# A two-layer decoder trunk on one core: a mask and its row count, PSUM pools and buffers of the two token mixers changed

## The chip, the cores and the metric

The kernel runs on one core of one Trainium2 chip. The metric is the device time of one execution in microseconds. Three executions of the kernel before took 2031.06, 2037.0 and 2038.48 us; their median is 2037.0.

## What is computed

x is 512 tokens by 1024, in float32. The reference runs two layers; each is half a feed-forward block, a token mixer, half a feed-forward block, and a layer norm after each of the three. The even layer's mixer is RG-LRU beside mLSTM, the odd layer's is RWKV-7 beside GLA.

```python
for l in range(DEPTH):
    x = layer_norm(alpha * x + 0.5 * swiglu_ffn(x, ffn1_wi[l], ffn1_wo[l]), ...)
    if l % 2 == 0:
        mix = even_mixer(x, ...)   # RG-LRU and mLSTM, one input and one output projection
    else:
        mix = odd_mixer(x, ...)    # RWKV-7 and GLA, likewise
    x = layer_norm(alpha * x + mix, ...)
    x = layer_norm(alpha * x + 0.5 * swiglu_ffn(x, ffn2_wi[l], ffn2_wo[l]), ...)
```

In the mLSTM part, a score between tokens i and j is weighted by exp of a gate difference, and j > i is masked out. RWKV-7 is a recurrence over tokens with a 64 x 64 state for each of 8 heads; GLA is a linear attention with 4 heads and a gate of its own.

## The kernel before

**Precision and weights.** Every large product is made of three: each float32 operand is split into a rounded part (hi) and the rest (lo), both of type float32r, and hi by hi, lo by hi and hi by lo are added in PSUM. `load` (L87) fetches 512 KB of weights into one of two `raw` buffers; `split` (L95) makes `whi` on ScalarE (L103) and `wlo` on VectorE (L107), or, in most of the odd mixer, on ScalarE (L105) and by an adding DMA (L110). There are five slots of each. `project_T` (L127) makes a projection of 128 outputs by 512 tokens with 16 products by whi (L132, L133) and 8 by wlo (L136); `project_N` (L148) does the same for four token tiles (L156 to L158).

**PSUM.** `psum` (L83) hands out banks of 128 x 512 from three pools: A has four buffers, B two, C two. An allocation takes a pool's buffers in turn, so it waits until the reader of the buffer's last use is done.

**Order.** A scheduler places the instructions of each engine. In the odd mixer `fill` (L658) also puts a number of steps of waiting projections (`filler`) in at marked places; the numbers are the table `FILL` (L25), one for each call of `fill` in the program's order. An engine works through its instructions in the order set.

**First mixer** (`even`, L318). The order is: `if` projection and four of the eight query and key projections (`pqk`) in two halves of 256 tokens, the other four in full (L433), each followed by a convolution of one step on ScalarE (L313) and three on VectorE (L316) that read the PSUM buffer; then the scores, the value projection (`pv`, L441), RG-LRU and the output. For one head and one block of 128 keys, `scores` (L414) makes a gate matrix `pr` of up to 512 columns in pool B. A product with 36 rows does it (L420): `sel` picks the head's row out of `Rs`, which holds 32 rows of hi parts and 4 of lo parts. A second product adds the mask (L421): the identity by a triangle of -1e30, both in bf16. ScalarE takes exp (L423), TensorE makes `pS` from keys and queries (L425), VectorE multiplies the two (L427). There are 16 such groups, mixed by the scheduler with the projections that follow.

**Second mixer** (`odd`, L567). RWKV-7 is handled in four blocks of 128 channels, two to a group. For each block, `keys` (L687) makes the decay product `pw` (L693) and the key gate product `pa` (L697), each with 32 rows, the norm `pn` (L706), which GpSimd raises to a power (L709), and a broadcast of it, `pi` (L732), after which VectorE builds `KRV` and `bk`. `bonus` (L740) makes `pb` with one more product. All of them use pool B, as `pl` does, the gate product of GLA (L933). Six buffers named `wk` hold what lies between. Then, for each group, `scores` (L746, `psc` L755), `inverse` (L786, 31 steps on VectorE between L792 and L801), `natural` (L762, transposes `ptk` and `ptb`, and `pz`), `merge` (L805, `pq`, `px`, `pwt`, `pu`) and `chain` (L850): eight chunks, one after another, in each of which `psa` (L864) reads the state that VectorE made from `pst` (L872) of the chunk before. GLA's projections (`pj`, `pv`, `po`, all in pool A) fill in.

**Second mixer, buffers of GLA's gates.** `gla_gates` (L928) takes four `wk` buffers for two channel blocks (`zb`, `za`), and the results go into the two buffers `ga`. `gwt` (L593), a 256-column weight, has a buffer of its own beside the `wk` pool.

Of the kernel before, what the change touches and what calls it, by code (L numbers as in the profile page):

```python
# [7 lines left out]
F32 = mybir.dt.float32  # L8
# [3 lines left out]
ALU = mybir.AluOpType  # L12
# [23 lines left out]
class Net:  # L36
# [281 lines left out]
    def even(self, l):  # L318
        nc, a, tc = self.nc, self.a, self.tc
        V, A, T, G = nc.vector, nc.scalar, nc.tensor, nc.gpsimd  # L320
        with tc.tile_pool(name="ev", bufs=1) as ep:
            bufs = dict(qk=8, row=4, wt=3, v=4, u=4, rg=6, o=6)

            def slot(tag, n=S):
                return ep.tile([P, 516 if tag == "v" else S], F32, name=tag, tag=tag, bufs=bufs[tag])[:, :n]
# [8 lines left out]
            msk = ep.tile([P, 2, P], BF, name="msk")  # L334
            mtmp = slot("wt", 256)
            nc.sync.dma_start(mtmp.rearrange("p (a b) -> p a b", a=2), a["c_mask_neg"])
            V.tensor_copy(out=msk, in_=mtmp.rearrange("p (a b) -> p a b", a=2))
# [52 lines left out]
            Rs = ep.tile([36, 1280], F32R, name="Rs")  # L390
            sel = ep.tile([36, 4], F32R, name="sel")
# [22 lines left out]
            def scores(h):  # L414
                pT = ep.tile([P, 1280], F32, name=f"pT{h}", tag="pT", bufs=4)
                out, off = [], 0
                for bj in range(4):
                    n = S - bj * P
                    pr = self.psum("pr")
                    T.matmul(pr[:, :n], sel[:, h:h + 1].broadcast_to([36, P]), R[bj], start=True, stop=False)  # L420
                    T.matmul(pr[:, :P], msk[:, 0, :], msk[:, 1, :], start=False, stop=True)  # L421
                    wt = slot("wt")
                    A.activation(wt[:, :n], pr[:, :n], AF.Exp, bias=cT[:, bj, h:h + 1])  # L423
                    pS = self.psum("pS")
                    T.matmul(pS[:, :n], qk[4 + h][:, bj * P:(bj + 1) * P], qk[h][:, bj * P:], start=True, stop=True)  # L425
                    o = pT[:, off:off + n]
                    V.scalar_tensor_tensor(out=o, in0=pS[:, :n], scalar=128 ** -0.5, in1=wt[:, :n], op0=ALU.mult, op1=ALU.mult)  # L427
                    out.append(o)
                    off += n
                return out  # L430


            for i in order[4:]:  # L433
                p_qk[i] = self.psum("pqk", "A")
                self.project_T(p_qk[i], self.weights())
                qk_tile(i)
# [130 lines left out]
    def odd(self, l):  # L567
# [6 lines left out]
        wk = tc.alloc_tile_pool(name="wk", bufs=6, side="right", reuse_waits="tile")  # L574
        with tc.tile_pool(name="od", bufs=1) as ep:
# [17 lines left out]
            gwt = wk.tile([80, 256], F32, name="gwt", bufs=1)  # L593
# [93 lines left out]
            def keys(ft, Dm, k, r, v):  # L687
# [4 lines left out]
                pw = self.psum("pw")  # L692
# [3 lines left out]
                pa = self.psum("pa")  # L696
# [43 lines left out]
            def bonus(ft, r, v):  # L740
                pb = self.psum("pb")
                T.matmul(pb, bones, r, start=True, stop=True)
                yT[ft] = slot("y")
                V.tensor_tensor(out=yT[ft], in0=v, in1=pb, op=ALU.mult)
# [183 lines left out]
            def gla_gates():  # L928

                zz = []  # L930
                for f in range(2):
                    pl = self.psum("pl")
                    T.matmul(pl, gw[:, f * P:(f + 1) * P], gd[0:80], start=True, stop=True)  # L933
                    zb, za = slot("wk"), slot("wk")
# [7 lines left out]
                for zb, za in zz:  # L942
                    V.scalar_tensor_tensor(out=zb, in0=zb, scalar=0.0, in1=za, op0=ALU.min, op1=ALU.add)
                    gbs.append(slot("ga"))
                    V.tensor_tensor_scan(out=gbs[-1], data0=reset, data1=zb, initial=0.0, op0=ALU.mult, op1=ALU.add)
# [230 lines left out]
def layouts(inp):  # L1176
# [45 lines left out]
    mk = np.zeros((P, 2, P), f)  # L1222
    mk[:, 0] = np.eye(P)
    mk[:, 1] = np.where(np.arange(P)[None, :] < np.arange(P)[:, None], -1e30, 0.0)
# [65 lines left out]
```

## Time and profile before

| | |
|---|---|
| median of three runs | 2037.0 us |
| profiled execution | 2036.15 us |
| its span in the trace | 2034.4 us |
| granted TensorE clock, mean | 0.993 |
| feed-forward block before the first mixer, from 0 to 375 us | TensorE busy 371.89 us |
| from 577 to 1342 us (two feed-forward blocks) | TensorE busy 764.42 us |
| from 1640 to the end | TensorE busy 385.59 us |

The profile is of one execution. Engines are PE (TensorE's products), PEld (its weight loads), DVE (VectorE), ACT (ScalarE), POOL (GpSimd) and SP (SyncE, which issues most DMAs). A row of the view in order of time gives the start, the duration, the engine, the line, the operation with out<-in and its shape, and in square brackets the idle time of the engine before it with what ended it. Products overlap, so TensorE's speed is read from the distance of starts, not from durations. A float32 product (not float32r) shows as two records, so its counts are twice those of the order of instructions. Page part 2 shows how the busy share and the clock run over the span, in 40 slices:

```profile
PE   9999999999999999999999999998999999999998
...
DVE  4332333776784333335533333466747683323335
ACT  4332332466424322332432233157635333322330
...
PEclk9999999999999999999999999998999999999999
```

The two stretches in which VectorE and ScalarE have high digits are the two mixers. TensorE is high throughout.

### The profile page before, as it was taken

To read this page: it belongs to the slowest core of one execution; us is meant where nothing else is said; L and a number is where in the kernel's file an instruction comes from. 1 tells how busy PE (TensorE), PEld (TensorE's weight loads), DVE (VectorE), ACT (ScalarE), POOL (GpSimd) and SP (SyncE) were. 2 spreads that over 40 slices of the span, in tenths; PEclk is the share of its full clock that TensorE was granted. 3 is DMA by queue.
4 is the path that set the end of the run, shared out by engine and by line. 5 is a ranking of instruction groups with operands and counts; after the bars stand their busy time and mean duration, and the time that the engine had idled before them with its cause. 6 is when DMAs were issued, how large, how long until landed. Compare 5 with 4: busy or idle time off the path is not lost. (4 is left out here: it accounts for less than half of the span.)

```text
span 2034.4 us, 26090 instructions
## 1 busy us (share of the span) xinstructions
PE 2008.5 (99%) x10499; PEld 1666.0 (82%) x10499; DVE 964.2 (47%) x1800; ACT 719.6 (35%) x1266; POOL 98.4 (5%) x159
## 2 busy tenths in 40 slices
PE   9999999999999999999999999998999999999998
PEld 8888888977889888888988888896778788888886
DVE  4332333776784333335533333466747683323335
ACT  4332332466424322332432233157635333322330
POOL 0000000100010000000000000012211200000001
PEclk9999999999999999999999999998999999999999
DMA  5333333332223323331433333254636023333331
GB/s 168 103 93 116 102 93 93 94 97 63 73 80 118 103 94 114 104 94 53 130 99 93 114 104 95 84 163 104 144 69 157 1 85 113 98 99 115 99 97 63
DMA packets 59482, 202.45 MB, mean 100 GB/s; under 512 B 7824, under 2 KB 8288, under 8 KB 59360
## 3 DMA queue, kind: packets, MB, share of 16 engines
q1 hardware_dynamic: 56336, 189.77, 30.2%
q0 software_dynamic: 3024, 11.01, 2.9%
q8 instruction: 82, 1.34, 0.3%
q14 instruction: 40, 0.33, 0.1%
HBM read 196.56 MB, written 4.19 MB: 99 GB/s over the span
## 5 line engine op out<-in xcount | busy, mean ns | idle before, releaser
L103 ACT ACTIVATE whi<-raw 128x512 fp32r<-128x512 f32 x661 | 379.6, 623 | 821.0 <-PE pgu L133 401.9
L107 DVE TENSOR_TENSOR wlo<-raw,whi 128x512 fp32r<-128x512 f32 x616 | 398.9, 687 | 541.4 <-ACT whi L103 515.5
L132 PE MATMUL pgu<-xh,whi 128*128 128x512 f32 (+1 forms) x1568 | 564.8, 369 | 1.5 <-ACT whi L103 1.2
L133 PE MATMUL pgu<-xl,whi 128*128 128x512 f32 (+1 forms) x1568 | 565.7, 368 | 0.0
L136 PE MATMUL pgu<-xh,wlo 128*128 128x512 f32 (+1 forms) x1568 | 353.7, 368 | 0.0
L132 PEld LDWEIGHTS pgu<-xh,whi 128*128 128x128 f32 x1568 | 295.3, 189 | 50.7 <-ACT whi L103 1.6
L133 PEld LDWEIGHTS pgu<-xl,whi 128*128 128x128 f32 x1568 | 296.4, 189 | 48.4
L136 PEld LDWEIGHTS pgu<-xh,wlo 128*128 128x128 f32 x1568 | 275.8, 189 | 48.6
L165 PE MATMUL acc<-whi,hh 128*128 128x512 f32 x704 | 274.6, 390 | 0.0
L166 PE MATMUL acc<-whi,hl 128*128 128x512 f32 x704 | 274.4, 390 | 0.0
L167 PE MATMUL acc<-wlo,hh 128*128 128x512 f32 x704 | 272.4, 390 | 0.0
L243 DVE TENSOR_TENSOR sg<-sg,pgu 128x512 f32<-128x512 f32 (+1 forms) x96 | 61.7, 643 | 336.5 <-PE pgu L136 332.8
L167 PEld LDWEIGHTS acc<-wlo,hh 128*128 128x128 f32 x704 | 132.2, 188 | 27.2
L165 PEld LDWEIGHTS acc<-whi,hh 128*128 128x128 f32 x704 | 132.2, 188 | 27.2
L166 PEld LDWEIGHTS acc<-whi,hl 128*128 128x128 f32 x704 | 132.2, 188 | 27.1
L170 ACT ACTIVATE hh<-sg 128x512 fp32r<-128x512 f32 (+1 forms) x96 | 57.2, 596 | 120.7 <-DVE sg L243 120.7
L200 POOL TENSOR_SCALAR rs<-mv 128x1 f32<-128x1 f32 x24 | 13.2, 548 | 1510.7 <-DVE mv L198 1510.7
L242 ACT ACTIVATE sg<-pgu 128x512 f32<-128x512 f32 (+1 forms) x96 | 53.7, 560 | 57.0 <-PE pgu L136 56.3
L170 ACT ACTIVATE xh<-pst 128x512 fp32r<-128x512 f32 x48 | 27.8, 597 | 108.3 <-PE pst L178 108.0
L132 PE MATMUL pj<-xh,whi 128*128 128x512 f32 (+2 forms) x184 | 63.2, 363 | 0.0
L171 DVE TENSOR_TENSOR hl<-sg,hh 128x512 fp32r<-128x512 f32 (+1 forms) x96 | 61.6, 642 | 0.6 <-ACT hh L170 0.5
L133 PE MATMUL pj<-xl,whi 128*128 128x512 f32 (+2 forms) x184 | 61.4, 351 | 0.0
(350 smaller groups left out, 2009.5 us busy)
## 6 DMA issues: line engine op xcount, KB each, us to landing
raw<-ffn_wi SPq DMA_DIRECT2D x176, 512.0 KB, 3.5
raw<-ffn_wo SPq DMA_DIRECT2D x88, 512.0 KB, 3.5
raw<-od_krv SPq DMA_DIRECT2D x12, 512.0 KB, 3.8
raw<-ev_qk SPq DMA_DIRECT2D x8, 512.0 KB, 3.6
raw<-ev_rg SPq DMA_DIRECT2D x8, 512.0 KB, 3.5
raw<-ev_w_out SPq DMA_DIRECT2D x8, 512.0 KB, 3.5
raw<-od_w_out SPq DMA_DIRECT2D x8, 512.0 KB, 4.2
wlo<-od_krv POOLq DMA_DIRECT2D x6, 512.0 KB, 7.1
```

Of the source, the lines that this page charges most:

```text
L103: self.nc.scalar.activation(hi[:, sl], t[:, sl], AF.Copy)
L107: self.nc.vector.tensor_tensor(out=lo[:, sl], in0=t[:, sl], in1=hi[:, sl].bitcast(F32), op=ALU.subtract)
L132: mm(o, hi[:, kt, :n], self.xh[:, kt, t0:t1], start=kt == 0, stop=False)
L133: mm(o, hi[:, kt, :n], self.xl[:, kt, t0:t1], start=False, stop=lo is None and kt == 7)
L136: mm(o, lo[:, kt, :n], self.xh[:, kt, t0:t1], start=False, stop=kt == 7)
L165: mm(o, ah, hi[:, cs], start=first and i == 0, stop=False)
L166: mm(o, al, hi[:, cs], start=False, stop=False)
L167: mm(o, ah, lo[:, cs], start=False, stop=last and i == len(lhs) - 1)
L170: self.nc.scalar.activation(hi, src, AF.Copy)
L171: self.nc.vector.tensor_tensor(out=lo, in0=src, in1=hi.bitcast(F32), op=ALU.subtract)
L242: nc.scalar.activation(sg, pp[f, 0][:, t0:t1], AF.Silu)
L243: nc.vector.tensor_tensor(out=sg, in0=sg, in1=pp[u][:, t0:t1], op=ALU.mult)
```

## The change

The first mixer: the mask becomes one 128 x 128 triangle of type float32r, and the identity by which it is multiplied is a float32r copy of the identity that is there already. `Rs` and `sel` grow from 36 to 128 rows; ScalarE fills rows 32 to 127 with zeros first (a constant scaled by 0), and rows 32 to 35 get their values afterwards, as before. So the product for `pr` has 128 rows, of which 92 are zero. The fifth and sixth projection for `pqk` take their PSUM buffers from pool C, and the last two take the next two of pool A.

The second mixer: `pw`, `pa`, `pb` and `pl` take PSUM buffers from pool A (four) and leave pool B (two) to `pn`, `pi` and what follows. There are seven `wk` buffers for six; `gwt` is one of them, no longer a buffer of its own; `zb` lies in a `ga` buffer and is worked on in place, so `gla_gates` needs two `wk` buffers for four. In `FILL` the number ahead of the last chunk's `psa` in the first group's chain goes from 0 to 2, and one in the second group's `natural` from 9 to 7.

```diff
-    3, 1, 2, 2, 3, 2, 1, 3, 2, 1, 0, 1, 1, 3, 0, 0, 6, 3, 3, 5, 6, 4, 2, 9, 0, 1, 17, 7, 5, 1, 2, 2,
+    3, 1, 2, 2, 3, 2, 1, 3, 2, 1, 2, 1, 1, 3, 0, 0, 6, 3, 3, 5, 6, 4, 2, 7, 0, 1, 17, 7, 5, 1, 2, 2,
...
-            msk = ep.tile([P, 2, P], BF, name="msk")
-            mtmp = slot("wt", 256)
-            nc.sync.dma_start(mtmp.rearrange("p (a b) -> p a b", a=2), a["c_mask_neg"])
-            V.tensor_copy(out=msk, in_=mtmp.rearrange("p (a b) -> p a b", a=2))
+            msk = ep.tile([P, P], F32R, name="msk")
+            mtmp = slot("wt", P)
+            nc.sync.dma_start(mtmp, a["c_mask_neg"])
+            V.tensor_copy(out=msk, in_=mtmp)
+            idr = ep.tile([P, P], F32R, name="idr")
+            V.tensor_copy(out=idr, in_=self.ident)
...
-            Rs = ep.tile([36, 1280], F32R, name="Rs")
-            sel = ep.tile([36, 4], F32R, name="sel")
+            Rs = ep.tile([P, 1280], F32R, name="Rs")
+            sel = ep.tile([P, 4], F32R, name="sel")
+
+            A.activation(Rs[32:64].rearrange("p (a b) -> p a b", a=10), self.expo[32:64].unsqueeze(2).broadcast_to([32, 10, P]), AF.Copy, scale=0.0)
+            A.activation(Rs[64:128].rearrange("p (a b) -> p a b", a=10), self.expo[64:128].unsqueeze(2).broadcast_to([64, 10, P]), AF.Copy, scale=0.0)
+            A.activation(sel[32:64], self.expo[32:64].broadcast_to([32, 4]), AF.Copy, scale=0.0)
+            A.activation(sel[64:128], self.expo[64:128].broadcast_to([64, 4]), AF.Copy, scale=0.0)
...
-                    T.matmul(pr[:, :n], sel[:, h:h + 1].broadcast_to([36, P]), R[bj], start=True, stop=False)
-                    T.matmul(pr[:, :P], msk[:, 0, :], msk[:, 1, :], start=False, stop=True)
+                    T.matmul(pr[:, :n], sel[:, h:h + 1].broadcast_to([P, P]), R[bj], start=True, stop=False)
+                    T.matmul(pr[:, :P], idr, msk, start=False, stop=True)
...
-                p_qk[i] = self.psum("pqk", "A")
+                p_qk[i] = self.psum("pqk", "C" if i in order[4:6] else "A")
...
-        wk = tc.alloc_tile_pool(name="wk", bufs=6, side="right", reuse_waits="tile")
+        wk = tc.alloc_tile_pool(name="wk", bufs=7, side="right", reuse_waits="tile")
...
-            gwt = wk.tile([80, 256], F32, name="gwt", bufs=1)
+            gwt = slot("wk")[:80, :256]
...
-                pw = self.psum("pw")
+                pw = self.psum("pw", "A")
...
-                pa = self.psum("pa")
+                pa = self.psum("pa", "A")
...
-                pb = self.psum("pb")
+                pb = self.psum("pb", "A")
...
-                    pl = self.psum("pl")
+                    pl = self.psum("pl", "A")
...
-                    zb, za = slot("wk"), slot("wk")
+                    zb, za = slot("ga"), slot("wk")
...
-                    gbs.append(slot("ga"))
-                    V.tensor_tensor_scan(out=gbs[-1], data0=reset, data1=zb, initial=0.0, op0=ALU.mult, op1=ALU.add)
+                    gbs.append(zb)
+                    V.tensor_tensor_scan(out=zb, data0=reset, data1=zb, initial=0.0, op0=ALU.mult, op1=ALU.add)
```

How the scheduler then sets TensorE's instructions, at three places. The first is in the first mixer, behind the last projection for `pqk`; - is before, + is the change, and L427, L428 and L432 are the former L420, L421 and L425:

```order
 L136 MATMUL pqk<-xh,wlo 128x512 x8
-L420 MATMUL pr<-Rs,sel 128x512
-L421 LDWEIGHTS msk
-L421 MATMUL pr<-msk 128x128
-L425 MATMUL pS<-qk 128x512
+L156 MATMUL pv<-whi,xh 128x512
+L157 MATMUL pv<-whi,xl 128x512
+L158 MATMUL pv<-wlo,xh 128x512
+L156 MATMUL pv<-whi,xh 128x512
+L427 MATMUL pr<-Rs,sel 128x512
+L428 MATMUL pr<-msk,idr 128x128
+L432 MATMUL pS<-qk 128x512
```

Four products of the value projection move ahead of the first `pr` group.

The second is in the second mixer, from the last products of the first group's scores to the first transposes, before:

```order
L693 MATMUL pw<-lt,lw 128x512
L755 MATMUL psc<-KRV,bk 128x128 x8
L136 MATMUL pj<-xh,wlo 128x512 x8
L697 MATMUL pa<-lt,lw 128x512
L755 MATMUL psc<-KRV,bk 128x128 x8
L706 MATMUL pn<-cst,wk 128x2 x4
L768 MATMUL ptk<-ident,KRV 128x128 x4
```

And in the change, where `psc` is L762 and `ptk` L775:

```order
L133 MATMUL pj<-xl,whi 128x512
L762 MATMUL psc<-KRV,bk 128x128 x8
L136 MATMUL pj<-xh,wlo 128x512 x8
L762 MATMUL psc<-KRV,bk 128x128 x8
L775 MATMUL ptk<-ident,KRV 128x128 x4
```

`pw`, `pa` and `pn` of the third block (block 2) are gone from here. They stand about 120 products later, on either side of the last projection ahead of `pq`, and `pi` and `pb` of that block behind `px`. There, in the change, the fourth block's (block 3's) products follow too; `pi` is L739, `pb` L749, `pw` L700, `pa` L704, `pwt` and `pu` L843, `pn` L713:

```order
L828 MATMUL px<-SC,WT 32x32 x32
L739 MATMUL pi<-ident,wk 128x128 x4
L749 MATMUL pb<-kr,cst 128x512
L700 MATMUL pw<-lt,lw 128x512
L704 MATMUL pa<-lt,lw 128x512
L132 MATMUL pj<-xh,whi 128x512
L133 MATMUL pj<-xl,whi 128x512
L136 MATMUL pj<-xh,wlo 128x512 x8
L843 MATMUL pwt<-SC,KV 64x64 x16
L843 MATMUL pu<-ZU,SC 64x64 x16
L713 MATMUL pn<-cst,wk 128x2 x4
```

Before, only block 3's `pi` and `pb` stood behind `px`; its `pw` and `pa` had been made beside the inverse.

The third is the end of the first group's chain, ahead of the last `psa`, before:

```order
L919 MATMUL pyt<-lt,lw 128x128 x2
L872 MATMUL pst<-KV,BK 128x128 x2
L864 MATMUL psa<-St,WT 128x128
L884 MATMUL py<-St,R 64x128
L888 MATMUL py<-KV,SC 64x64
```

In the change (`pst` is L879, `psa` L871):

```order
L926 MATMUL pyt<-lt,lw 128x128 x2
L879 MATMUL pst<-KV,BK 128x128 x2
L156 MATMUL pv<-whi,xh 128x512
L157 MATMUL pv<-whi,xl 128x512
L158 MATMUL pv<-wlo,xh 128x512
L156 MATMUL pv<-whi,xh 128x512
L157 MATMUL pv<-whi,xl 128x512
L158 MATMUL pv<-wlo,xh 128x512
L871 MATMUL psa<-St,WT 128x128
```

Six value products move in between `pst` and `psa`.

More of the change, by code (lines that the diff above doesn't have):

```diff
@@ L1221, in layouts @@
     o["c_ident"] = np.eye(P, dtype=f)
-    mk = np.zeros((P, 2, P), f)
-    mk[:, 0] = np.eye(P)
-    mk[:, 1] = np.where(np.arange(P)[None, :] < np.arange(P)[:, None], -1e30, 0.0)
+    mk = np.where(np.arange(P)[None, :] < np.arange(P)[:, None], f(-1e30), f(0))
     o["c_mask_neg"] = mk
```

## The prediction

> **What bounds the kernel now.** I read the page first, then the busy time by stage, then the granted clock in short stretches, then TensorE's instructions in order of time. Part 1 of the page:
>
> ```profile
> PE 2008.5 (99%) x10499; PEld 1666.0 (82%) x10499; DVE 964.2 (47%) x1800; ACT 719.6 (35%) x1266; POOL 98.4 (5%) x159
> ```
>
> The busy time by stage (window, its length, busy time and instructions of each engine, granted clock, DMA share, GB/s), the first mixer and then the second:
>
> ```profile
> 375.00:577.00 202.00, 199.84 (x1000) 160.14 (x999) 142.39 (x297) 111.56 (x183) 7.06 (x13) 0.99 0.32 95
> ...
> 1342.00:1640.00 298.00, 286.76 (x2233) 224.88 (x2232) 192.92 (x490) 159.36 (x304) 59.98 (x94) 0.97 0.43 105
> ```
>
> TensorE bounds nearly everything, so a microsecond is won only where it stands between two of its starts: a wait, a slow pair, or a time at half clock. The feed-forward stages are not touched; only these two windows can move. Within them the clock falls four times (same columns; the first row is the stretch before a fall):
>
> ```profile
> 416.00:419.30 3.30, 1.39 (x9) 1.06 (x9) 3.30 (x6) 1.69 (x3) 0.00 (x0) 1.00 0.42 149
> 419.50:422.70 3.20, 3.20 (x9) 2.52 (x8) 3.20 (x9) 3.17 (x7) 0.00 (x0) 0.50 0.55 164
> ...
> 1382.10:1388.60 6.50, 6.50 (x19) 4.00 (x18) 4.01 (x7) 4.12 (x8) 0.54 (x2) 0.50 1.03 240
> ...
> 1412.80:1419.40 6.60, 5.94 (x25) 5.45 (x25) 4.56 (x8) 6.48 (x13) 2.01 (x3) 0.50 0.63 137
> ...
> 1508.40:1515.00 6.60, 6.60 (x33) 4.67 (x32) 2.49 (x8) 1.42 (x3) 0.00 (x0) 0.50 0.01 2
> ```
>
> PE was busy 1.39 of 3.30 us, and then the clock is 0.50 for 3.4 us. Each fall costs half of its length: about 1.6, 3.4, 3.4 and 3.4 us. The sum below starts at the profiled execution, 2036.15 us (span 2034.4 and 1.75 around it), 0.85 under the median of 2037.0.
>
> **The change, part by part.**
>
> *128 rows and the float32r mask.* TensorE in order of time (start, duration), one group of the first mixer:
>
> ```profile
> 454.51 0.39 PE L158 MATMUL pv<-wlo,xh 128*128 128x512 f32 x1
> 454.74 0.39 PE L156 MATMUL pv<-whi,xh 128*128 128x512 f32 x1
> 455.05 0.50 PE L420 MATMUL pr<-Rs,sel 36*128 36x512 f32 x1
> 455.48 0.23 PE L421 MATMUL pr<-msk 128*128 128x128 bf16 x1
> 455.52 0.48 PE L157 MATMUL pv<-whi,xl 128*128 128x512 f32 x1
> 455.84 0.39 PE L158 MATMUL pv<-wlo,xh 128*128 128x512 f32 x1
> ```
>
> Full-array steps come every 0.23 us. Around the 36-row product the intervals are 0.31, 0.43, 0.04 and 0.32, together 1.10. With 128 rows I take 0.23, 0.23, then the mask, then 0.23. No row shows a float32r product of 128 columns. It is bounded by a quarter of 0.23 (0.06) and by a transpose of that shape, 0.12:
>
> ```profile
> 1398.43 0.66 PE L732 MATMUL pi<-ident,wk 128*128 128x128 f32 x4
> 1398.92 1.02 PE L742 MATMUL pb<-kr,cst 128*128 128x512 f32 x2
> ```
>
> (0.49 for four). I take 0.11, nearer the transpose. That gives 0.80, a saving of **0.30** a group; what goes is not streaming time, so I take it for the shorter groups too: 16 x 0.30 = **4.8 us**. The bounds are 0, if the excess belongs to this product and not to its row count, and 16 x 0.36 = 5.8. The Trainium skill's "TensorEngine Tiling (Array Packing)", Key Properties, says that a change of tiling mode drains the engine; the 0.43 beside 0.23 agrees. One rule speaks against the change, and its row is this:
>
> ```profile
> L421 PEld LDWEIGHTS <-msk x16: 95/96/97, 431.6 to 524.4; 128*128 128x128 bf16 x16
> ```
>
> The Trainium skill's "TensorE: Matmul & The Clock Gate", Weight-path perf modes, gives fast weight loads to 128 weights that are not FP32, and the new mask loses that. By that rule alone 16 loads grow by some 0.09, 1.4 us if none is hidden, and the time would be that much higher.
>
> The four new fills of Rs and sel stand on ScalarE ahead of this row:
>
> ```profile
> 388.80 0.21 ACT L456 ACTIVATE tm<-pc 128x4 f32<-128x4 f32 x1 [2.92 <-DMA pc<-ev_pc]
> ```
>
> Two fills of 1280 columns and two small ones, some 2.9 us as an estimate from the 0.6 us that this engine takes for 512 columns (L103 in the page's groups), fit into that wait; they cost nothing, or 0.3 us if the cast of xh behind them slips. VectorE's second copy, beside a smaller mask cast, lies in the same stretch and is costed at nothing.
>
> *Two projections elsewhere.* The third of the last four projections waits for a pool-A buffer:
>
> ```profile
> 416.09 0.46 PE L409 MATMUL pct<-ident,row 64*128 64x64 f32 x4
> 418.46 0.47 PE L132 MATMUL pqk<-xh,whi 128*128 128x512 f32 x1 [1.91 <-DVE qk L316]
> ```
>
> That wait and the fall behind it go: 1.9 + 1.6, and some 0.2 of restart, 3.7 us. What is late next is the value projection, whose third and fourth accumulators now reuse the buffers of the last two projections and so wait for their convolutions. VectorE's busy time there (fifth number), then the end of these convolutions and TensorE's place, in order of time:
>
> ```profile
> 415.00:425.00 10.00, 8.09 (x32) 6.18 (x31) 9.97 (x21) 6.80 (x12) 0.00 (x0) 0.83 0.34 108
> ```
>
> ```profile
> 431.32 1.29 DVE L107 TENSOR_TENSOR wlo<-raw,whi 128x512 fp32r<-128x512 f32 x2 [1.09 <-ACT whi L103]
> ...
> 434.68 1.52 DVE L316 SCALAR_TENSOR_TENSOR qk<-pqk,pc,qk 128x510 f32<-128x510 f32 x2
> ```
>
> ```profile
> 431.15 0.50 PE L420 MATMUL pr<-Rs,sel 36*128 36x512 f32 x1
> ...
> 436.47 0.39 PE L156 MATMUL pv<-whi,xh 128*128 128x512 f32 x1
> ```
>
> VectorE was busy 9.97 of 10 us, so its convolutions move up only by the 1.09 of idleness: the last ends near 435.1, not 436.2 (434.68 + 1.52), and the one before it two steps of 0.7 earlier, near 433.6. TensorE ends the projections 3.7 earlier, at 427.4. Ahead of the third accumulator stand 12 value products (2.7), one pr group (0.34) and pS (0.86): it is reached near 431.3, and a new wait of 2.3 opens. The fourth starts one accumulator (6 x 0.23) later, at 435.0 instead of 436.5: 1.5 earlier, of which 0.3 is the pr group's, counted already. That leaves about **1.3 us** of the 3.7; the bounds are -0.3 (the clock falls there, 1.6) and 3.7.
>
> *The pool of four, first half.* TensorE from the first bonus (pb) to the first transpose (ptk):
>
> ```profile
> 1377.66 1.02 PE L742 MATMUL pb<-kr,cst 128*128 128x512 f32 x2
> 1379.26 1.12 PE L693 MATMUL pw<-lt,lw 32*128 32x512 f32 x2 [0.57 <-DVE wk L734]
> 1381.38 1.56 PE L755 MATMUL psc<-KRV,bk 64*128 64x128 f32 x16 [1.00 <-DVE bk L737]
> 1382.87 2.07 PE L697 MATMUL pa<-lt,lw 32*128 32x512 f32 x2
> ...
> 1401.18 1.10 PE L933 MATMUL pl<-ga,gw 80*128 80x512 f32 x2 [1.24 <-DVE wk L734]
> ...
> 1413.46 1.87 PE L706 MATMUL pn<-cst,wk 128*128 128x2 f32 x8 [2.92 <-ACT wk L702]
> 1415.19 1.10 PE L768 MATMUL ptk<-ident,KRV 128*128 128x128 f32 x4
> ```
>
> These are 37.5 us. The waits of 0.57, 1.00, 1.24 and 2.92 (5.7) go: pw, pa and pl no longer ask for the two buffers that pi and pn hold, and pn of block 2 no longer stands here. So does the part of the third fall in which TensorE worked before 1415.19 (1.7 us at half clock, 0.9). pw, pa and pn of block 2 move behind the inverse and are counted there (1.1, 1.1, and half of pn's 1.73 at half clock: 3.1). Two waits stay or come. psc still waits for bk, near 1381.4; with pw and pa ahead of it TensorE is there at 1380.7: 0.7. And pn of block 1 now stands two products behind psc, near 1382.9, and reads a square that ScalarE makes in turn:
>
> ```profile
> 1381.26 0.68 ACT L695 ACTIVATE wk<-pw,pc 128x512 f32<-128x512 f32 x1
> ```
>
> This tanh, a copy, pa's tanh and the square, 0.6 to 0.7 each, end near 1383.9: 1.0. The fall at 1382 I leave in, since pw, pa, psc and pn still stand close together. 37.5 - 3.1 - 5.7 - 0.9 + 1.7 = 29.5, so **4.9 us** for equal work (37.5 - 3.1 - 29.5). The bounds: 2, if each removed wait leaves half of itself behind, and 8.3, if the fall at 1382 goes too.
>
> *Second half, to the first chain step.* The 31-step inverse on VectorE, and TensorE behind it:
>
> ```profile
> 1416.67 1.98 DVE L792 STREAM_TRANSPOSE ZU<-SC 64x1024 f32<-64x1024 f32 x1 [0.24 <-ACT SC L760]
> ...
> 1457.56 1.91 DVE L801 STREAM_TRANSPOSE SC<-ZU 64x1024 f32<-64x1024 f32 x1
> ```
>
> ```profile
> 1429.04 1.12 PE L693 MATMUL pw<-lt,lw 32*128 32x512 f32 x2
> ...
> 1458.71 1.20 PE L814 MATMUL pq<-WT,SC 32*32 32x32 f32 x64
> ...
> 1466.38 0.66 PE L732 MATMUL pi<-ident,wk 128*128 128x128 f32 x4 [0.35 <-ACT wk L730]
> ...
> 1474.30 0.71 PE L864 MATMUL psa<-St,WT 128*128 128x128 f32 x4
> ```
>
> Before, from ptk (1415.19) to psa, 59.1 us. Gone are half of the 4.3 us at half clock (2.1) and pi's wait of 0.35. The inverse starts earlier, about as TensorE does, so pq is met in step. But blocks 2 and 3 now run around the merge instead of beside the inverse, with fewer projections to cover px, pi and pb. From the end of L801 (1459.5) to pi it was 6.9 us, through VectorE, GpSimd and ScalarE. In the new order TensorE stands at pi after pq, ten projection products and px (1.1 + 2.3 + 1.1), 2.7 after L801: a wait of up to 4.2. One DMA issue fewer stands ahead of GpSimd's power in its queue, so I take 3.0 (bounds 1 and 4.2), and 1.7 for one short fall among so many products of 32 rows. -2.1 - 0.35 + 3.0 + 1.7 is 2.2 us more. First and second half together: 4.9 - 2.2 = **2.7**.
>
> *Two value steps.* Before the last chain step:
>
> ```profile
> 1506.53 0.46 PE L864 MATMUL psa<-St,WT 128*128 128x128 f32 x2 [1.29 <-DVE St L877]
> ```
>
> Six value products of 0.23 (1.4 us) now stand in this wait; they are missing ahead of a transpose of the next group, where other value and output products still stand around it, so I cost that at nothing (1.4 if that cover is gone). The wait goes, 1.4, and with TensorE busy the fall of 1508, 3.4: **4.8**.
>
> Sum: 4.8 + 1.3 + 2.7 + 4.8 = 13.6; 2036.15 - 13.6 = 2022.55, given as **2022.5**.
>
> **The rivals.**
> - *The clock stays full.* If none of the new waits costs clock, the 3.4 at 1382 and the 1.7 fall away: 2017.4. Against it stands the row at 416, where 1.91 us of idleness was enough. The Trainium skill's "TensorE: Matmul & The Clock Gate", What's actually happening, has the clock fall after an idle window of some 3.4 us. By that rule this rival would hold, as every new wait is shorter; the trace disagrees, with 1.91.
> - *The falls move.* The new wait at 431 and the merge are as idle as 416, and the chain step stays a small-product stretch: 1.6 + 1.7 + 3.4 come back: 2029.2. For it speak the four falls, all among such products.
> - *The second mixer gives nothing.* The waits only change their names, and the chain stays as it is: 4.8 + 1.3 are left, 2030.0. For it: the inverse, not PSUM, sets the date of pq.
> - *The 36 rows were not the cause.* 4.8 less: 2027.3. Against it: three odd intervals beside every such group.
> - *Slower.* Block 3's pw now stands behind px. If its way to pi takes as long as now, 1429.0 to 1466.4 or 37.3 us, TensorE stands before pi, with the chain queued behind: by the new order it gets there 13 us after pw (two products of pw and pa, some 26 of 0.23, four small groups and pn), so it waits 24: 2046.5. It decides from a wait of 13.6. Against it: most of those 37 us were the inverse, which is over by then.
>
> **How the numbers follow.** Forecast 0.45 (its own range 2017 to 2027), full clock 0.12, falls move 0.20, second mixer nothing 0.11, rows not the cause 0.06, slower 0.06. 0.5%, about what a measurement can tell from no change, is 10.2 us: below 2026. Faster: nearly all of the forecast's 0.45, the 0.12, and 0.08 of the two cases near the line: 0.65. Same: 0.29. Slower: 0.06. The range reaches down to 2013 (full clock, 2017.4, less 1.0 for the mask at its cheapest, 2.4 for the first mixer's upper bound and some of the 2.0 of waits at pi) and up to 2032 (second mixer nothing, and a fall in the first, 1.6); it leaves out the slower case and some tails.
>
> **What would show it.** Right: intervals near 0.23 around pr and no 0.43; no wait at pqk but one of 2 at pv near 431; no wait at pl and none of 2.9 at pn; full clock behind the last chain step. Wrong: 0.43 still there at 128 rows; waits of 5 us and more at pi, pn or px; half clock at more places than two; a wait of VectorE on TensorE between 412 and 431, which would break the 2.3.

## The result, and the profile after

The change makes the kernel faster: 2019.97 us median of 6 runs (2017.57 to 2023.2) against 2037.74 for the kernel before beside it; the ratio is 0.9919, with a 95% interval of 0.9907 to 0.9931. That is 16.5 us (14 to 19 by the interval, counted at 2037) where 13.6 were forecast. The profiled execution took 2018.88 us, its span is 2017.1. Page part 1 of the kernel after, then the busy time by stage (window, its length, busy time and instructions of each engine, granted clock, DMA share, GB/s) for the first mixer, the two places of half clock that have gone, and the one that is new:

```profile
PE 1991.7 (99%) x10499; PEld 1658.8 (82%) x10499; DVE 962.4 (48%) x1801; ACT 725.1 (36%) x1272; POOL 99.8 (5%) x159
```

```profile
375.00:577.00 202.00, 199.88 (x1026) 165.72 (x1025) 148.51 (x307) 117.64 (x189) 8.80 (x15) 1.00 0.31 95
416.00:419.30 3.30, 3.30 (x17) 2.49 (x16) 3.30 (x7) 1.81 (x4) 0.00 (x0) 1.00 0.39 138
...
1354.40:1357.60 3.20, 3.04 (x8) 1.83 (x7) 1.37 (x3) 3.20 (x7) 1.75 (x3) 0.50 0.83 210
1375.00:1420.00 45.00, 40.74 (x286) 31.59 (x283) 32.86 (x65) 35.38 (x61) 9.06 (x10) 1.00 0.50 104
...
1490.00:1510.00 20.00, 20.00 (x145) 15.88 (x146) 11.39 (x37) 7.62 (x18) 3.58 (x7) 1.00 0.41 85
```

The instructions of TensorE are as many as before (10499). The clock is full at 416, from 1375 to 1420 and around the last chain step, where before had its four falls; the one fall that the mixers have left, at 1354, stands where before had none. The waits of TensorE in the second mixer (who waits, for whom, us in total, times, longest):

```profile
PE ptk L775 <- DVE SC L764: 2.6, 1, 2.6
PE pj L132 <- DVE kr L619: 1.8, 2, 1.7
...
PE pn L713 <- ACT wk L709: 0.7, 1, 0.7
...
PE px L828 <- DVE WT L823: 0.5, 1, 0.5
PE pb L749 <- POOL kr L734: 0.4, 1, 0.4
```

pl and psc wait no more, pn 0.7 for 2.92. New waits stand ahead of ptk, pj and ptb (1.0, not in the lines above). In sum TensorE waits as long as before in the second mixer: the waits of this view are 10.8 us before and 11.3 after. Cut at the starts of the same products, the two profiled executions differ so (us):

| stretch | before | after | gained | forecast |
|---|---|---|---|---|
| TensorE's first product to the first pqk | 375.3 | 374.0 | 1.3 | 0 |
| first pqk to the first pr or pv | 54.7 | 51.6 | 3.0 | 3.7 |
| from there to the first pyt (16 pr groups) | 126.8 | 122.9 | 3.8 | 2.4 (4.8 less 2.4) |
| first pyt to the second mixer's first pw | 800.7 | 801.1 | -0.4 | 0 |
| first pw to the first psa | 115.7 | 110.1 | 5.6 | 2.7 |
| first psa to the last | 140.5 | 136.6 | 3.9 | 4.8 |
| from there to TensorE's last product | 411.0 | 410.9 | 0 | 0 |

The first row is no work of the change. TensorE's fourth product of the feed-forward block, before and after, in order of time:

```profile
10.73 0.42 PE L133 MATMUL pgu<-xl,whi 128*128 128x256 f32 x1
```

```profile
10.54 0.28 PE L133 MATMUL pgu<-xl,whi 128*128 128x256 f32 x1
```

Before takes half as long again, and its clock is on record as full only from 13.2 us; after had full clock from 9.5. The date at which the clock comes up differs from execution to execution (3.9 to 13.5 us in the 14 traces of this study), and the first pqk comes 373.6 us into the span where it is early and 376.6 where it is late, so 1.3 us of the 17.3 by which the two spans differ are chance.

### The profile page after: what moved, and what is told of

Same layout as the page of the kernel before. It is cut to its first block, busy times and chain, and to the rows that moved or that the text cites. A ratio compares the mean times of both kernels' runs of the same rounds, so it can differ in the third digit from the quotient of the medians.

```text
span 2017.1 us, 26089 instructions
## 1 busy us (share of the span) xinstructions
PE 1991.7 (99%) x10499; PEld 1658.8 (82%) x10499; DVE 962.4 (48%) x1801; ACT 725.1 (36%) x1272; POOL 99.8 (5%) x159
## 4 chain that ended last, share of the span: by engine, by line
PE 93%; ACT 3%; DVE 2%; DMA 1%; issue 1%; POOL 0%; POOLq 0%; DVEq 0%; SPq 0%; ACTq 0%
PE pgu L132 16%; PE pgu L133 16%; PE pgu L136 16%; PE acc L165 8%; PE acc L167 8%; PE acc L166 8%; PE pout L165 1%; PE pj L132 1%; PE pout L166 1%; PE pout L167 1%; PE pj L133 1%; PE pj L136 1%; PE pst L178 1%; PE pv L156 1%; PE po L156 1%; PE pv L157 1%
## 5 line engine op out<-in xcount | busy, mean ns | idle before, releaser
L166 PEld LDWEIGHTS acc<-whi,hl 128*128 128x128 f32 x704 | 132.2, 188 | 27.1
L170 ACT ACTIVATE hh<-sg 128x512 fp32r<-128x512 f32 (+1 forms) x96 | 57.2, 596 | 121.1 <-DVE sg L243 121.1
L200 POOL TENSOR_SCALAR rs<-mv 128x1 f32<-128x1 f32 x24 | 13.2, 549 | 1509.2 <-DVE mv L198 1509.2
L170 ACT ACTIVATE xh<-pst 128x512 fp32r<-128x512 f32 x48 | 27.8, 597 | 108.4 <-PE pst L178 108.4
```

The source lines that it names most:

```text
L166: mm(o, al, hi[:, cs], start=False, stop=False)
L170: self.nc.scalar.activation(hi, src, AF.Copy)
```

## The experiments

All times of the runs stand here. "Half-clock loss" is worked out from each run's span and mean granted clock (span times one minus the clock) and averaged over the runs of a kernel; since that clock has three decimals, a single run is good to 1 us either way only. The loss has two limits: the start of the program, where no clock is on record, is not in it, and some 2 us of it stand at the end of every trace, behind TensorE's last product, where half clock costs nothing. Differences between kernels are not touched by the second. The last column is the mean time less this loss. Each ratio is to runs of before made beside that kernel; those beside the last six rows have a loss of 14.4 or 14.0 and 2020.4 or 2020.5 without it.

| kernel | median, us | ratio to before, 95% interval | half-clock loss | mean time without it |
|---|---|---|---|---|
| before (31 runs) | 2035.9 | | 15.0 | 2020.4 |
| after | 2020.0 | 0.9919, 0.9907 to 0.9931 | 6.1 | 2014.3 |
| rows_alone | 2031.8 | 0.9983, 0.9970 to 0.9996 | 15.4 | 2016.5 |
| pqk_alone | 2036.9 | 1.0011, 0.9995 to 1.0027 | 17.7 | 2020.1 |
| pool_alone | 2032.0 | 0.9978, 0.9967 to 0.9990 | 12.4 | 2019.4 |
| fill_alone | 2028.4 | 0.9964, 0.9950 to 0.9978 | 9.1 | 2018.9 |
| after_same_rows | 2020.2 | 0.9928, 0.9905 to 0.9952 | 5.6 | 2014.7 |
| after_old_fill | 2025.1 | 0.9949, 0.9933 to 0.9965 | 8.7 | 2016.0 |
| after_old_projections | 2023.7 | 0.9938, 0.9919 to 0.9957 | 7.7 | 2014.8 |
| spare_128_rows | 2032.7 | 0.9986, 0.9974 to 0.9998 | 10.2 | 2021.7 |
| spare_1_row | 2034.6 | 0.9995, 0.9985 to 1.0006 | 14.1 | 2020.1 |
| block0_pool_b | 2018.7 | 0.9920, 0.9903 to 0.9937 | 8.1 | 2010.7 |

By these means the gain of the whole is 15.0 us: 8.9 of half clock (15.0 to 6.1) and 6.1 of all else. mask_36_rows and rows128_bf16 are read by the trace alone (one execution each, 2036.2 and 2035.1 us).

### Each part alone, on the kernel before

rows_alone takes the hunks of `msk`, `idr`, `Rs`, `sel` and `pr`, pqk_alone the line of `p_qk[i]`, pool_alone those of pw, pa, pb, pl, `wk`, `gwt` and `zb`, and fill_alone the two numbers:

```
-3, 1, 2, 2, 3, 2, 1, 3, 2, 1, 0, 1, 1, 3, 0, 0, 6, 3, 3, 5, 6, 4, 2, 9,
+3, 1, 2, 2, 3, 2, 1, 3, 2, 1, 2, 1, 1, 3, 0, 0, 6, 3, 3, 5, 6, 4, 2, 7,
```

> The kernel before with only the 128 rows and the float32r mask. If the 36 rows caused the odd intervals: 0.23, 0.23, 0.06 and 0.28 around the wide pr groups (0.80 for 1.10), 4.6 us less between the last query-key product and the first transpose of the first mixer, and a time lower by 4 to 5 us (ratio near 0.998); the wait of 1.9 at the third projection and its half clock stay, as do the falls in the second mixer. If the type of the mask caused them, the same numbers come out and the two runs that split rows from type have to tell. If the 0.29 a group is taken back by a later wait (value products, copies of the mask), the intervals shorten and the stretch does not: under 2 us.

Measured: the stretch of the 16 groups falls from 126.75 to 123.06 (3.7), the time by 3.5 (0.0017 of 2036); half clock is as before (15.4 for 15.0). The falls at 420, 1379, 1410 and 1505 are all there.

> The kernel before with only the two projections in pool C. By the order of the value products as the trace after shows it (two accumulators worked through three weight tiles, 34 products, before the third accumulator is touched) no wait opens at the third accumulator, and all of the 1.9 wait and of the half clock go: 3.0 to 3.5 us from the first query-key product to the last. By the prediction's rule (12 products ahead of the third accumulator) a wait of 2.3 opens near 431 and about 1.3 us are left. If the fall of the clock only moves, 1.9.

Measured: 50.9 for 54.7 in its own stretch (3.8 gained), no wait and no half clock there, and nothing lost behind it (126.81 for 126.75). The value products open no wait. Yet the time did not fall: the interval holds no change, and the half-clock loss is 17.7 for 15.0 (one of the 12 runs, 2050.4 us at a clock of 0.986, stands far above the others). In the profiled execution the second mixer, whose instructions are those of before, has four falls up to psa for two. How the length of that stretch goes with them, in the eight traces that have the old second mixer up to psa:

| half clock between the first pw and the first psa, us | length of the stretch, us |
|---|---|
| 6.8 (mask_36_rows) | 112.4 |
| 13.7 (six kernels) | 115.2 to 116.6 |
| 23.9 (pqk_alone) | 121.1 |

From the first row to the last that is 8.7 us for 17.1 of half clock: half of a fall's length, the price that the prediction used. So the same instructions take 112 to 121 us by chance of the clock, and a part worth 3 us can vanish in that. Whether the second mixer's extra falls in this kernel are only chance stays open.

> The kernel before with pw, pa, pb and pl in the pool of four, seven work buffers and zb in place; nothing of the first mixer, and the filler numbers of before. Theory one, the prediction's: it gains by waits and half clock that go (0.57, 1.00, 1.24, 2.92), with 2 to 3 us left of the stretch from pw to the first psa. Theory two: pw and pa, with 32 rows each of different rows of the array, stand side by side and run at the same time, each of the four pairs in 1.06 us where 2.1 were needed one after the other; then the four pairs take 4.3 us of starts, where pw and pa of before took 9.4, and the stretch gains 5 us or more. Half clock in the stretch from 1376 to 1420 is gone by both.

Measured: 111.1 for 115.7 in the stretch, and 4.5 us in the time by the ratio; by the means it is 3.7, 2.6 of it in the half-clock loss and 1.0 in all else. That lies between the numbers of the two theories. The half clock of the first is most of it: it falls from 13.7 to 6.8 us, which at half its length is 3.4 of the 4.6. Its waits are not: the named ones go, but TensorE is idle for 7.0 us in the stretch, where before it was 6.7. The pairs do run side by side (below).

> The kernel before with only the two filler numbers. If the fall behind the last chain step comes from the thin work there, six value products of 0.23 us in front of psa keep the clock full behind it: the wait of 1.29 goes, 3.4 us of half clock go, less what is missing later, 4 to 5 us in the stretch from the first psa to the last. If the fall comes anyway (it has its own dates), it stands a few us earlier or later and 1.4 or less is won.

Measured: 135.8 for 140.5 in the stretch from the first psa to the last, no fall there, and 7.3 us in the time, the largest of the four. 5.9 of it is half clock (15.0 to 9.1). By their ratios the four parts alone give 3.5, -2.2, 4.5 and 7.3, together 13.1 of the 16.5; the intervals are wide enough for the difference.

### Rows or type of the mask

Both on the kernel before; the first takes the hunk of the mask, the second that of `Rs` and `sel`:

```
 mask_36_rows:
-T.matmul(pr[:, :P], msk[:, 0, :], msk[:, 1, :], start=False, stop=True)
+T.matmul(pr[:, :P], idr, msk, start=False, stop=True)
 rows128_bf16:
-T.matmul(pr[:, :n], sel[:, h:h + 1].broadcast_to([36, P]), R[bj], start=True, stop=False)
+T.matmul(pr[:, :n], sel[:, h:h + 1].broadcast_to([P, P]), R[bj], start=True, stop=False)
```

> The kernel before with the float32r mask, and still 36 rows. If the rows cause the odd intervals (a change between a product of 36 rows and one of 128 costs time on either side): 0.32 ahead of pr and some 0.43 behind it stay, and the group of pr and mask is 1.05 to 1.15 as before. If the bf16 mask between float32r products causes them: 0.80 as after, with 36 rows.

> The kernel before with 128 rows, and still the bf16 mask. If the rows cause the odd intervals: 0.23, 0.23, 0.04 and 0.28 or so, 0.75 to 0.80 a group. If the type of the mask does: 1.05 to 1.15. If each has a half: near 0.95.

TensorE in order of time around a wide group (start, duration), first 36 rows with the float32r mask, then 128 rows with the bf16 mask, then the kernel after:

```profile
453.77 0.39 PE L156 MATMUL pv<-whi,xh 128*128 128x512 f32 x1
454.09 0.50 PE L422 MATMUL pr<-Rs,sel 36*128 36x512 f32 x1
454.52 0.33 PE L423 MATMUL pr<-msk,idr 128*128 128x128 f32 x1
454.68 0.45 PE L157 MATMUL pv<-whi,xl 128*128 128x512 f32 x1
454.96 0.39 PE L158 MATMUL pv<-wlo,xh 128*128 128x512 f32 x1
```

```profile
453.60 0.39 PE L156 MATMUL pv<-whi,xh 128*128 128x512 f32 x1
453.83 0.40 PE L425 MATMUL pr<-Rs,sel 128*128 128x512 f32 x1
454.07 0.23 PE L426 MATMUL pr<-msk 128*128 128x128 bf16 x1
454.11 0.48 PE L157 MATMUL pv<-whi,xl 128*128 128x512 f32 x1
454.42 0.40 PE L158 MATMUL pv<-wlo,xh 128*128 128x512 f32 x1
```

```profile
448.12 0.40 PE L157 MATMUL pv<-whi,xl 128*128 128x512 f32 x1
448.36 0.40 PE L427 MATMUL pr<-Rs,sel 128*128 128x512 f32 x1
448.59 0.22 PE L428 MATMUL pr<-msk,idr 128*128 128x128 f32 x1
448.65 0.45 PE L158 MATMUL pv<-wlo,xh 128*128 128x512 f32 x1
448.94 0.40 PE L156 MATMUL pv<-whi,xh 128*128 128x512 f32 x1
```

The distances of starts are 0.32, 0.43, 0.16, 0.28 (1.19) with 36 rows and float32r; 0.23, 0.24, 0.04, 0.31 (0.82) with 128 rows and bf16; 0.24, 0.23, 0.06, 0.29 (0.82 in this group, 0.81 in the others of its width) after, where before had 0.31, 0.43, 0.04, 0.32 (1.10). The rows cause all of the 0.29. The new type of the mask is worth about nothing at 128 rows and would have cost 0.09 a group at 36.

### pw and pa side by side

```
-T.matmul(pa, lw[32:64, cs], lt[32:64], start=True, stop=True)
+T.matmul(pa, lw[0:32, cs], lt[0:32], start=True, stop=True)
```

> The kernel after, in which pa takes rows 0 to 31 of its operands in the place of rows 32 to 63 (its values are then not those of the reference), in the same order on every engine. If pw and pa gain because they stand side by side on different rows of the array and run together, each of the four pairs now takes 2.1 us and not 1.06: four times 1.06, 4.2 us more of starts on TensorE, of which up to 4.2 is seen in the stretch from pw to psa (2 to 3 if waits behind them shrink). If the pairs gained for another reason (the pool alone), nothing changes: 0 to 0.5.

The same pair in order of time, after, and then with the same rows (a float32 product shows as two records):

```profile
1374.36 0.69 PE L700 MATMUL pw<-lt,lw 32*128 32x512 f32 x1
1374.37 0.69 PE L704 MATMUL pa<-lt,lw 32*128 32x512 f32 x1
1374.90 0.59 PE L700 MATMUL pw<-lt,lw 32*128 32x512 f32 x1
1374.90 0.59 PE L704 MATMUL pa<-lt,lw 32*128 32x512 f32 x1
1375.42 1.16 PE L762 MATMUL psc<-KRV,bk 64*128 64x128 f32 x16
```

```profile
1374.17 1.12 PE L700 MATMUL pw<-lt,lw 32*128 32x512 f32 x2
1375.13 1.02 PE L704 MATMUL pa<-lt,lw 32*128 32x512 f32 x2
1376.08 0.60 PE L762 MATMUL psc<-KRV,bk 64*128 64x128 f32 x6
```

Rows 0 to 31 and rows 32 to 63 run at the same time: pw and pa together take 1.06, with the same rows 1.91. Over the four pairs that is 3.4 us of TensorE. Little of it reaches the time: the stretch is 2.2 longer, and this execution has a fall at 1402 that the other has not (3.4 of half clock, up to 1.7); the wait at pn (0.7) and that at px (0.5) are gone from its waits. The medians are 2020.2 and 2020.0. Without half of each fall the two stretches are 108.8 and 108.4. So the pairs do run side by side, and in the time no gain from it can be told: the ratios are 0.9928 (0.9905 to 0.9952) and 0.9919.

### The value steps and the projections taken back out

after_old_fill is the kernel after with the old line of numbers, after_old_projections the kernel after with `self.psum("pqk", "A")` for all.

> The kernel after with the two filler numbers of before. If a stretch of 3.4 us in which the array is used, rows counted, to under about 0.38 brings half clock in the next, as in 18 of the 20 falls of the traces so far: the one ahead of the last chain step is that thin again, half clock of 6.8 to 13.7 us comes back behind it (3.4 to 6.8 us) with the wait of 1.2, and the time rises by 5 to 8 us (ratio to the kernel before 0.994 to 0.996, for 0.992). If the new order of the second mixer has kept the clock up by itself, 1 to 2 us.

Measured: the time rises by 5.1 in the median, 6 by the ratios (0.9949 for 0.9919). In the trace half clock of 13.7 us stands behind 1498, and the stretch from the first psa to the last is 143.9 for 136.6. The new order of the second mixer did not keep the clock up by itself.

> The kernel after with all four late projections in pool A again. If what the run with this part alone lost again was chance of the clock (falls elsewhere, in a second mixer that stood on the edge): here, where the second mixer is off that edge, the wait of 1.9 and mostly its fall come back, 3 to 4 us between the first query-key product and the last, and the time rises by 2.5 to 4. If the wait's gain is always paid back later: no change in time, and the stretch behind it shorter by as much.

Measured: 2023.7, 3.7 more in the median, though the intervals of the two ratios overlap (0.9919 to 0.9957 and 0.9907 to 0.9931). The wait of 1.9 is back. In this execution no fall follows it (53.1 for 51.6 in the stretch), and the second mixer has two falls more. Its direction agrees with a gain of 3 us for this part in the changed kernel; the size is not settled.

### Six spare products ahead of the last chain step

The kernel has a helper `busy` that issues products into a buffer which is overwritten next. On the kernel before, with no work moved (r is 1 in spare_1_row):

```
-ys = list(chain(old))
+ys = list(chain(old, {("psa", 7): 6}))
 spare_1_row, besides:
-T.matmul(p, self.xh[:, 2, :P], self.xh[:, 3, :], start=True, stop=True)
+T.matmul(p, self.xh[:r, 2, :P], self.xh[:r, 3, :], start=True, stop=True)
```

> The kernel before with its old filler numbers, and six products of 128 rows whose result nobody reads (they go into the buffer that psa overwrites) in the wait ahead of the last chain step of the first group. No work is moved and none is saved. If half clock behind that step comes from a thin stretch of 3.4 us ahead of it (share of the array used, rows counted, 0.36 to 0.37 in all eight traces with the old numbers): six times 0.23 raise it to about 0.75, the clock stays full from 1495 to 1530, the stretch from the first psa to the last takes 135 to 138 us for 140.5 to 143.9, and the time falls by 4 to 7 us, though there are more instructions. If the value steps of the change gained by filling the wait and not by the clock: 0 to 1 us slower than before.

> The same six products at the same place in the same order, but of one row. They keep TensorE busy for as long. If the clock goes by rows (row share rises by under 0.01, so stays near 0.37): the fall behind the last chain step stays, 6.8 to 13.7 us of half clock, and the time is that of before within 1 us or up to 1 us more. If it goes by busy time alone: as with 128 rows, 4 to 7 us less.

The six products as one row in order of time, and two windows (columns as above; the first is 3.4 us long and holds them, the second is what follows), with 128 rows and then with one:

```profile
1502.29 1.62 PE L848 MATMUL psa<-xh 128*128 128x512 f32 x6
```

```profile
1501.00:1504.40 3.40, 3.40 (x22) 2.59 (x21) 2.16 (x8) 1.44 (x4) 0.14 (x1) 1.00 0.59 116
1504.40:1511.20 6.80, 6.80 (x56) 5.18 (x54) 3.63 (x15) 1.46 (x4) 0.00 (x0) 1.00 0.01 2
```

```profile
1504.06 1.66 PE L848 MATMUL psa<-xh 1*128 1x512 f32 x6
```

```profile
1503.72:1507.13 3.41, 3.41 (x20) 2.50 (x18) 1.96 (x8) 0.46 (x2) 0.00 (x0) 1.00 0.25 48
1507.20:1513.90 6.70, 6.70 (x37) 4.85 (x36) 2.41 (x7) 1.42 (x3) 0.00 (x0) 0.50 0.01 2
```

In both, TensorE is busy for the whole of the first window. On the grid of each trace's falls, the stretch of 3.41 us that holds them uses the array to 0.73 with 128 rows and to 0.28 with one, rows counted (the last section says how). With 128 rows the clock stays full; with one row it falls to 0.50 for 6.8 us, as in the kernel before. The stretch from the first psa to the last is 137.3 with 128 rows and 140.5 with one (140.5 before). Useless work makes the kernel faster, though only just clear of no change: 0.9986, whose interval ends at 0.9998. The half-clock loss is 10.2 against 14.1 with one row and 14.0 in the runs of before beside it. The gain is smaller than expected (2.9 for 4 to 7); by the last column of the table the six products cost some 1.2 themselves (2021.7 for 2020.5 without the loss).

### Block 0 back in the pool of two

```
-pw = self.psum("pw", "A")
+pw = self.psum("pw", "A" if ft else "B")
-pa = self.psum("pa", "A")
+pa = self.psum("pa", "A" if ft else "B")
```

> The kernel after, with pw and pa of the first block back in the pool of two (those of blocks 1 to 3 stay in the pool of four). After, these two take two of the four buffers of which the projections behind them need one: TensorE waits 1.7 for a convolution, and the only fall of the mixers stands behind it (half clock for 3.4, 1.7). If that is so: no wait at that place, no fall near 1354, 3 us less from the first pw to the first psa (107 for 110), time 2016 to 2018. If the inverse on VectorE sets the date of the merge anyway: the wait goes, and a wait at ptk or pq takes its place; under 1.5 us.

After, in order of time, the wait that this takes away:

```profile
1353.63 0.50 PE L132 MATMUL pj<-xh,whi 128*128 128x512 f32 x1 [1.67 <-DVE kr L619]
```

It is gone, and so is the fall at 1354; a wait of 1.2 at psc takes part of its place, and a fall of 3.4 stands at 1371. The stretch is 108.3 for 110.1, the span of this execution 2013.2 for 2017.1. By the time it can't be told from the kernel after (2018.7 and 2020.0, ratios 0.9920 and 0.9919); without the half-clock loss it is 3.6 lower, the lowest of all. So the first theory holds in part: the wait and its fall go, but a fall comes elsewhere, and the stretch gains 1.8 where 3 were expected.

## Why the prediction was nearly right

The time lies within the range and 2.5 us below the forecast. The terms one by one:

- **128 rows: forecast 4.8, measured 4.6 in the groups and 3.8 in the stretch.** The groups of the four widths gain 0.29, 0.31, 0.30 and 0.25, 4.6 for the 16; the mask took 0.06 where 0.11 was assumed (0.11 in the narrowest groups), and the product behind it 0.28 where 0.23 was. 3.7 to 3.8 of it is left in the stretch; of the rest, 0.5 is a wait of pS for VectorE in the trace after. That the rows and not the type are the cause is shown by mask_36_rows and rows128_bf16. The fills on ScalarE took 2.9, as estimated. The slower weight loads that the prediction set beside its sum are there: the load of the mask product's weights took 0.096 us with bf16 and takes 0.187 now.

```profile
L428 PEld LDWEIGHTS pr<-msk,idr x16: 187/188/188, 427.7 to 517.2; 128*128 128x128 f32 x16
```

But they are hidden. At 128 rows the wide groups take 0.82 with the bf16 mask and 0.81 to 0.82 with the new one; only the four narrowest differ, 0.65 and 0.68, some 0.1 us in all for the 1.4.
- **Two projections: forecast 1.3, measured 3.0.** The step that failed is "Ahead of the third accumulator stand 12 value products". In the changed order 34 value products, on the first two accumulators, stand ahead of the third. The last convolutions on VectorE and the third accumulator's first product on TensorE, in the kernel after:

```profile
431.92 2.18 DVE L316 SCALAR_TENSOR_TENSOR qk<-pqk,pc,qk 128x509 f32<-128x509 f32 x3
```

```profile
436.19 0.92 PE L156 MATMUL pv<-whi,xh 128*128 128x512 f32 x2
```

The first of the three (one is 0.74) frees the third accumulator's buffer at 432.7, and TensorE comes for it with the second product of its row, at 436.7, without a wait ahead of it: the wait of 2.3 never opens. VectorE's dates were right (the last convolution was forecast for 435.1 and ends at 434.1 in an execution that is 1.3 us ahead); TensorE's order had not been followed far enough. The wait and its fall went whole, 3.8 in pqk_alone; the 3.0 here hold a wait of the `if` projection for xh that was 0.7 longer than before, and that is 0.2 to 1.7 in the 14 traces.
- **Second mixer: forecast 2.7, measured 5.6.** The number is half of what was measured, and the mechanism is another. The terms of the forecast and the trace, from the first pw to the first psa (us; half clock at half its length):

| | before | after | change | forecast change |
|---|---|---|---|---|
| TensorE idle | 6.7 | 7.2 | +0.5 | -1.4 (-5.7 - 0.35 + 1.7 + 3.0) |
| half clock | 6.8 | 1.7 | -5.1 | -1.3 (-0.9 - 2.1 + 1.7) |
| the rest | 102.2 | 101.2 | -1.0 | 0 |

The step that failed is that the gain comes from waits: those of 5.7 went, the largest of them down to 0.7, and others of the same size took their place, at ptk (2.6), pj (1.7) and ptb (1.0). Waits of 3.0 were put at px, pi and pb and are 0.7, 0 and 0.4. The clock, which was to fall twice in the new order, fell once, at another place, and that made nearly all of the gain. The rest is of the size of the pairs of pw and pa, which were priced one after the other and run together. By halves, the one up to ptk was put at 29.5 from 37.5 and took 27.1, the one behind it at 64.4 and took 60.4; ahead of pb 3.6 were lost that no term held, the wait of 1.7 at pj and half of the fall behind it. The slower rival's long way of block 3's pw to pi does not happen: pi waits for nothing. And the 5.6 is itself in part chance of the clock: in the four kernels that have this part of the change whole (after, pool_alone, after_old_fill, after_old_projections) the stretch took 110.1, 111.1, 112.3 and 114.7, with 3.4 to 13.7 us of half clock, 112.1 in the mean; in the eight with the old one it took 115.9 in the mean. By these, one trace of each kernel, the gain is 3.9.
- **Value steps: forecast 4.8, 3.9 in the profile, 7.3 alone.** The mechanism (work in a thin stretch keeps the clock full) is what the spare products show. The size was taken from one execution: the fall behind the last chain step was 6.8 us there, and 6.8 to 13.7 in the eight traces that have it, 11.5 in the mean. 1.4 and half of 11.5 is 7.2.
- **The rivals.** In the profiled execution the falls did not move to the places named, and the second mixer gave more than nothing. But "The falls move" was more than a thought: in pool_alone, after_old_fill and after_old_projections, which have the same second mixer up to psa, falls stand at the merge (from 1445 to 1459). "The clock stays full" (2017.4) came nearest on the clock, with one fall left for none. By the Trainium skill's "TensorE: Matmul & The Clock Gate", What's actually happening, the clock falls after an idle window of some 3.4 us; the trace of spare_1_row contradicts that, since TensorE was busy for 3.41 of 3.41 us there, and the clock fell.

The prediction had right what the 36 rows cost, why the value steps gain, and the price of a fall, half of its length. That the sum came within 2.5 us is partly luck: in the profiled pair two terms were too small (1.3 and 2.7) and two too large (both 4.8), and in the second mixer the clock gave what the waits did not.

## What to carry to other kernels

Where TensorE sets the time, read the granted clock in stretches of a few us beside the waits: a thin stretch costs half of the fall behind it, which can be more than the wait that made it, and moving a few full-array products into it wins both back. A small gain is judged by its own stretch in the trace as well as by the time, since falls at other places move the time of the same instructions by several us; and the stretch of one execution is still one draw of the clock. A wait that goes is no gain until the waits of the whole stretch are summed: here waits of 5.7 us went, and TensorE was idle for as long as before. Before a new wait is priced, follow the waiting engine's order up to the waiting instruction itself, to the last accumulator and not to where a pattern seems to lead.

## What the runs showed of the hardware

**The clock falls where few rows of the array are in use, on a grid.** Every fall inside the mixers is a multiple of 3.41 us long (3.4, 6.8, 10.2, 13.7). For each of the 14 traces the stretches of 3.41 us in the mixers, on the grid of its falls, were weighed: each product by the time in which its columns stream (0.227 us for 512 columns of float32r, twice that for a record of a float32 product) times its rows over 128, as a share of 3.41. What followed a stretch at full clock:

| share of the array used, rows counted | stretches | half clock behind them |
|---|---|---|
| under 0.38 | 38 | 38 |
| 0.38 to 0.50 | 38 | 3 |
| 0.50 to 0.70 | 200 | 3 |
| over 0.70 | 1673 | 0 |

Near the limits the counts move by a few with the details of the weighing. The streaming time without the rows does not separate them: stretches of over 0.8 (pqk_alone, and spare_1_row, whose share with the rows is 0.28), with products of few rows, were followed by half clock, and two of 0.40, all with 128 rows, were not. Nor do the rows alone settle it: the three falls behind 0.63 to 0.65 stand at the merge, among products of 32 x 32 and 64 x 64. With the columns in use counted too, these have 0.36 to 0.38 and no fall is left above 0.5, but then several stretches of 0.35 to 0.38 have no half clock behind them. Which measure the clock goes by stays open; that the rows count is shown. A wait of 1.9 that brings half clock in one execution and none in another fits: where the grid cuts it, no stretch is thin enough (0.44 ahead of 418 in pool_alone, no fall). The spare products of 128 and of one row are the test by intervention; the table is an observation. What lets the clock come back after 3.4 us in one place and after 13.7 in another was not tried. The Trainium skill's "TensorE: Matmul & The Clock Gate", What's actually happening, states a free-running window of 3413 ns; the lengths agree.

**A product of 36 rows between products of 128 costs time on either side** (0.09 us ahead, 0.20 behind, at 512 columns), while two products of 32 rows that lie in different rows of the array cost one: 1.06 us for pw and pa together.
